# A gated pooling and forgetting-attention block: copies moved to ScalarE's queue, a store deferred, V's transposes in another bank, buffers shifted by 128 bytes, and another pacing

## The chip, the cores and the metric

The kernel runs on one core of one Trainium2 chip. The metric is device time in microseconds (us) of one execution. A core has five engines that run their own instruction streams in order: TensorE (PE, matmuls; its weight loads are listed apart as PEld), VectorE (DVE), ScalarE (ACT), GpSimd (POOL) and SyncE (SP, which here only issues DMA transfers). They meet through semaphores. The profile also gives the clock that was granted to TensorE, as a share of full speed.

## The reference

One hybrid decoder block on 1024 tokens of width 1024, with 16 learned meta tokens put ahead of them, all in float32:

```python
h = rmsnorm(concat(meta, x), norm_g)
u_pool, z_pool, q, k, v, z_attn, f_logit, g_pool, g_attn = split(h @ w_in)
y_pool = causal_multiscale_pool(u_pool, pool_w, pool_scale) * silu(z_pool)
log_f = log_sigmoid(f_logit + b_forget)
# 8 heads of 64; logit[t, s] = q_t.k_s / 8 + sum of log_f over s < j <= t, causal, softmax
y_attn = forgetting_attention(q, k, v, log_f) * silu(z_attn)
merged = sigmoid(g_pool) * (y_pool @ w_up_pool) + sigmoid(g_attn) * (y_attn @ w_up_attn)
out = rmsnorm(h_in + merged @ w_out, final_norm_g)[:, 16:]
```

## The kernel before

**Numbers.** Each operand of a large matmul is split into a rounded high part and the rest (hi and lo), and a product is three matmuls: hi by hi, hi by lo, lo by hi (`g_mm3`, L167). ACT makes the high parts (L158), POOL most low parts (L160).

**Stages.** First the normalised input is transposed into `hh` and `hl` (hi and lo) and the first pair of heads gets its q, k and v. Then comes attention, up to about 442 us of the profiled execution. After it come the gate products (L1034), the two up-projections (`up`, L1234) and the output product (`prod`, L1350). The gate products and the output product are a seven-product scheme on quarter matrices of 512 by 512, so that sums and differences of quarters are needed. These sums are made in DRAM during attention: a copy puts one quarter into a *sum buffer* (`GS`, `TD`, `HS`), and an adding transfer issued by POOL adds another (`add`, L609). `SUMS` (L639) lists by unit which copies (`put`, `put_g`, `put_h`, and `put_neg`, which first negates a block of the input) and additions are issued.

**Attention.** It is cut into 16 units: four pairs of heads, two heads each, two halves of 512 queries. A unit has 5 blocks of 128 keys (first half) or 9 (second half); blocks on the diagonal are narrower. For each block, `qk` (L689) makes the scores in a PSUM bank, which ACT and DVE move to the tile S with bias and mask, and DVE keeps a running maximum. `maxes` (L720) turns that into one maximum per query, with two 32-by-32 transposes on DVE and small copies on ACT. `soft` (L739) subtracts the maximum (DVE), takes the exponential (ACT), splits it into ph (ACT) and pl (DVE), and adds it into `acc` for the row sums (POOL). `av` (L762) multiplies ph and pl by V, two blocks later. The score blocks of unit i+1 are merged with the softmax blocks of unit i (`merged`, L782). At the end of a unit `finish` (L769) stores the output and `acc`.

**Filler.** PE's order is written out by the program. Between attention's blocks a filler (`Fill`, L370) hands PE projections: q, k, v of the next pair of heads, which must be done by a given unit, and others that are stored for later (u and gates, `f_u` L358 and `f_raw` L348; their results go through the two `st` buffers to DRAM). After each block, `merged` calls `F.pull(PACE * dve - pe)`: `dve` is the planner's estimate of the VectorE time of that block in ns, `pe` the TensorE time of the block, and the filler then issues matmuls of that nominal duration (`mm_ns`). Further pulls stand around the maxima (`LM1`, `LM2`) and ahead of a unit's last two `av` (`TAIL`). The order on the other engines is made by the scheduler of the framework from the program's order, its dependences and hand-written orders (`after`).

**Banks.** Of the eight PSUM banks, `pj` has two, `pk` one, `psT` two, `psS` two, `psO` one. During attention the projections alternate over the two of `pj` (`fill_bank`, L183, with `spare` false), and the scores over the two of `psS` and the one of `pk` (`third`, L177). V is projected transposed in three pieces of columns (`f_v`, L337), and blocks of it are turned by TensorE (`v_blocks`, L308) into a bank taken by `fill_bank`.

**Memory.** SBUF is given out in order: `cst`, `wp` (weight splits), `gp` (q, k and other large tiles), `stg` (the `st` buffers), `sm` (small), then `ap` (attention: S, V, acc, ph, pl) and later in its place `bp` (gate weights `gw`, za, zp and others). `hh` and `hl`, and later `hq` (operands of the later products), lie at the other end. `PADS` puts unused bytes into `cst` (`lead`) and `sm` (`rest`).

Of the kernel before, what the change touches and what calls it, by code (L numbers as in the profile page):

```python
# [22 lines left out]
KB = 128  # L23
# [4 lines left out]
COL_F, COL_GP, COL_GA = 3072, 3080, 4104  # L28
PIECES = ((0, 384), (384, 768), (768, 1040))
HROW = 1088  # L30
PADS = {"lead": 32, "rest": 0}
HALVES = ((0, 512), (512, 1024))
PJ, PT = 2, 2
PACE = 1.05
LATENCY = 1800.0
LAT2 = 1600.0
LM1, LM2 = 1400.0, 1800.0
TAIL = 900.0
FIRST = 2200.0
NPH = 3  # L40
LAG = 2
# [9 lines left out]
def mm_ns(n):  # L51
    return max(n * 0.4219, 107.0)
# [3 lines left out]
def tile_hybrid_block(ctx, tc, x, meta, norm_g, w_in, b_forget, pool_w, pool_scale,  # L56
                      w_up_pool, w_up_attn, w_out, final_g, out):
    nc = tc.nc
# [124 lines left out]
    def fill_bank():  # L183
        return third(pj, "pj") if spare[0] else pj.tile([128, 512], F32, name="pj")
# [121 lines left out]
            V[p, e] = ap_.tile([KB, NB, 2, 64], F32R, name="V", bufs=3)  # L306

    def v_blocks(p, *parts):  # L308
        pt = fill_bank().rearrange("p (n e d) -> p n e d", e=2, d=64)
        n = 0  # L310
        for b0, b1 in parts:
            for b in range(b0, b1):
                nc.tensor.transpose(pt[:, n], VT[p][:, KS[b]:KS[b] + KB], ident)
                n += 1
                yield 109.0
        for e in range(2):
            n = 0
            for b0, b1 in parts:
                pv = pt[:, n:n + b1 - b0]
                n += b1 - b0  # L320
                vh = V[p, e][:, b0:b1, e, :]
                nc.scalar.activation(vh, pv[:, :, e, :], AF.Copy)
                nc.vector.tensor_tensor(V[p, e][:, b0:b1, 1 - e, :], pv[:, :, e, :], r32(vh), op=ALU.subtract)
# [89 lines left out]
    F = Fill()  # L413
# [185 lines left out]
    def rows_of(t):  # L599
        return t.rearrange("(k p) c -> p k c", p=128)  # L600

    def put(dst, src):
        after(nc.sync.dma_start(dst, src), stores[-1])

    def put_g(dst, src):
# [13 lines left out]
    def put_neg(blk, k, *dsts):  # L619
        t = ap_.tile([128, 512], F32, name="neg", bufs=2)  # L620
        after(nc.scalar.activation(t, hblock(hh4, blk)[:, k], AF.Copy, scale=-1.0), exps[-1])
        for c in range(0, 512, 256):
            sub = nc.gpsimd.tensor_tensor(t[:, c:c + 256], t[:, c:c + 256], hblock(hl4, blk)[:, k, c:c + 256],
                                          op=ALU.subtract)
            after(sub, accs[-1])
        for d in dsts:
            put(HS[d][128 * k:128 * k + 128], t)

    def n21(k):
        put_neg("21", k, "X", "A")  # L630
# [38 lines left out]
    class Unit:  # L669
# [9 lines left out]
        def a_steps(self):  # L679
            for b in range(self.nb):  # L680
                w = 512 - self.c0[b]
                yield w, 0.8 * w + 110 + 250 * (b * KB + KB > self.t0), 2 * mm_ns(w), (lambda b=b: self.qk(b))

        def c_steps(self):
            for b in range(self.nb):
                w = 512 - self.c0[b]
                yield w, 2.8 * w + 390, 2 * mm_ns(w), (lambda b=b: self.soft(b))

        def qk(self, b):  # L689
            p, e, q0, t0, kb, c0 = self.p, self.e, self.q0, self.t0, self.kb[b], self.c0[b]  # L690
# [48 lines left out]
        def soft(self, b):  # L739
            kb, c0 = self.kb[b], self.c0[b]  # L740
            s = self.S[b]
            if b == 0:
                self.po = psO.tile([128, 512], F32, name="po")
                self.acc = ap_.tile([KB, 512], F32, name="acc", bufs=2)
            nc.vector.tensor_tensor(s[:kb, c0:], s[:kb, c0:], self.pm[:kb, c0:], op=ALU.subtract)  # L745
            exps.append(nc.scalar.activation(s[:kb, c0:], s[:kb, c0:], AF.Exp))  # L746
            ph = ap_.tile([128, 512], F32R, name="ph", bufs=NPH)
            pl = ap_.tile([128, 512], F32R, name="pl", bufs=NPH)
            nc.scalar.activation(ph[:kb, c0:], s[:kb, c0:], AF.Copy)  # L749
            dves.append(nc.vector.tensor_tensor(pl[:kb, c0:], s[:kb, c0:], r32(ph[:kb, c0:]), op=ALU.subtract))  # L750
            self.P[b] = (ph, pl)
            acc, S0 = self.acc, self.S[0]
            if b == 1:
                if c0:
                    nc.gpsimd.tensor_copy(acc[:, :c0], S0[:, :c0])
                accs.append(nc.gpsimd.tensor_tensor(acc[:, c0:], S0[:, c0:], s[:, c0:], op=ALU.add))  # L756
            elif b > 1:
                accs.append(nc.gpsimd.tensor_tensor(acc[:kb, c0:], acc[:kb, c0:], s[:kb, c0:], op=ALU.add))  # L758
            if b >= LAG:
                self.av(b - LAG)  # L760
# [8 lines left out]
        def finish(self):  # L769
            hr, lr = rows(self.e)  # L770
            po, acc = self.po, self.acc
            t = ap_.tile([128, 512], F32, name="t")
            if self.p == 3:
                nc.scalar.activation(t[hr], po[lr], AF.Copy)
                nc.vector.tensor_tensor(t[hr], po[hr], t[hr], op=ALU.add)
            else:
                nc.scalar.activation(t, po, AF.Copy)
            for n, part in (("y", hr), ("y2", lr))[:1 if self.p == 3 else 2]:
                nc.sync.dma_start(spill[n, self.p][hr, self.q0:self.q0 + 512], t[part])
            nc.sync.dma_start(accd[:, 4 * self.p + 2 * self.e + self.half], acc)  # L780

    def merged(a, c):  # L782
        out_ = []
# [37 lines left out]
    for i, u in enumerate(units):  # L821
        nxt = units[i + 1] if i + 1 < 16 else None
        F.now = i
        if nxt is not None and nxt.p != u.p:
            F.until(f"q{nxt.p}", f"k{nxt.p}")
        merged(list(nxt.a_steps()) if nxt else [], list(u.c_steps()))
        for b in range(u.nb - LAG, u.nb):
            F.pull(TAIL)
            u.av(b)
        if i == 1:  # L830
            after(nc.scalar.activation(pwh, pw, AF.Copy), exps[-1])
            nc.gpsimd.tensor_tensor(pwl, pw, r32(pwh), op=ALU.subtract)
        if nxt is not None:
            nxt.maxes(hook=lambda tr: sums_at(i, tr))
        u.finish()
        if i == 12:
            g_raw0 = [gp.tile([128, 2, 512], F32, name="graw", tag="g") for _ in range(2)]
            for k in range(2):
                put(g_raw0[k], rows_of(GSRC[0][0])[:, 2 * k:2 * k + 2])
        if i == 14:  # L840
            g_w0 = [[gp.tile([128, 2, 512], F32R, name="gw0", tag="g") for _ in range(2)] for _ in range(2)]
            for k in range(2):
                after(nc.scalar.activation(g_w0[0][k], g_raw0[k], AF.Copy), exps[-1])
                for c in range(0, 2):
                    for h0 in (0, 256):
                        after(nc.gpsimd.tensor_tensor(g_w0[1][k][:, c, h0:h0 + 256], g_raw0[k][:, c, h0:h0 + 256],
                                                      r32(g_w0[0][k][:, c, h0:h0 + 256]), op=ALU.subtract), accs[-1])
        if nxt is not None and nxt.p != u.p:
            F.until(f"v{nxt.p}")
            pair_fill(nxt.p + 1)  # L850
    F.drain()
    last_dve = dves[-1]
    A.close()
# [620 lines left out]
```

## Time and profile before

| what | value |
|---|---|
| time, median of 3 runs | 741.27 us (741.16 to 744.6) |
| time of the profiled execution | 742.0 us |
| its span, first to last instruction | 740.3 us |
| mean granted TensorE clock | 0.993 |
| PE busy | 714.7 us (97%) |
| PEld busy | 612.2 us (83%) |
| DVE busy | 521.7 us (70%) |
| ACT busy | 426.3 us (58%) |
| POOL busy | 336.2 us (45%) |
| DMA | 134.08 MB, mean 181 GB/s |

Busy time of PE includes the overlap of matmuls that follow each other in the pipeline, so a matmul's listed mean (some 390 ns at 512 columns) is longer than the distance to the next one. A window row gives the stretch, then for each engine its busy us and instructions (x), then the granted clock, the share of the DMA engines and GB/s. A group row gives line, engine, operation, output and inputs, shape, count, then busy us and mean ns of one, then the engine's idle time before it and what ended it. A timeline row gives start, duration and instruction, with the idle time before it in brackets. A chain row gives start, duration and group.

### The profile page before, as it was taken

How to read it: one execution, taken by the hardware profiler on the slowest of the kernel's cores; microseconds unless marked ns; L12 is line 12 of the kernel's file. 1: busy time of each engine (PE TensorE's matmuls, PEld its weight loads, DVE VectorE, ACT ScalarE, POOL GpSimd, SP SyncE). 2: the span in 40 equal slices, each digit the busy share in tenths (PEclk: the TensorE clock that was granted, in tenths of full speed). 3: DMA queues.
4: the chain of work that ended last, by engine and by line, in shares of the span. 5: the costliest groups of instructions: out<-in, count | busy, mean ns of one | idle time of the engine just before them, and what ended most of it. 6: DMA issues, size and time to landing. Idle time of an engine off the chain costs nothing.

```text
span 740.3 us, 10889 instructions
## 1 busy us (share of the span) xinstructions
PE 714.7 (97%) x3613; PEld 612.2 (83%) x3613; DVE 521.7 (70%) x917; ACT 426.3 (58%) x944; POOL 336.2 (45%) x417
## 2 busy tenths in 40 slices
PE   8999999698999899998999999999999999999996
PEld 6997999597779888897788887888888888888885
DVE  5743479376777867888686894889756654887775
ACT  7653477465796766776666733436544522626445
POOL 5412337446465764657356763355953011006243
PEclk9999999899999999999999999999999999999998
DMA  9211252854989759494888879889605557672006
GB/s 303 60 29 30 73 167 89 247 141 140 300 227 244 197 143 248 128 283 124 234 219 215 224 182 349 298 220 328 182 28 178 177 185 268 218 270 69 0 1 227
DMA packets 97226, 134.08 MB, mean 181 GB/s; under 512 B 11569, under 2 KB 62769, under 8 KB 94914
## 3 DMA queue, kind: packets, MB, share of 16 engines
q1 hardware_dynamic: 93360, 112.42, 47.5%
q0 software_dynamic: 2512, 18.35, 12.9%
q10 hardware_dynamic: 1298, 2.63, 0.9%
q8 instruction: 28, 0.46, 0.2%
q14 instruction: 28, 0.23, 0.1%
HBM read 103.29 MB, written 62.59 MB: 224 GB/s over the span
## 4 chain that ended last, share of the span: by engine, by line
PE 72%; ACT 9%; DVE 7%; DMA 2%; issue 2%; POOL 1%; POOLq 0%; SPq 0%; ACTq 0%; DVEq 0%
PE pj L172 38%; PE pj L1034 12%; PE pj L1354 8%; PE pt L1034 4%; PE po L766 4%; PE pt L1354 2%; ACT S L746 2%; DMA sp_u<-st 2%; ACT ph L749 1%; PE ps L705 1%; PE ps L704 1%; ACT S L709 1%; PE pj L529 1%; DVE pl L750 1%; DVE S L745 1%
## 5 line engine op out<-in xcount | busy, mean ns | idle before, releaser
L172 PE MATMUL pj<-hh,whi 128*128 128x512 f32 (+3 forms) x576 | 130.5, 354 | 7.9 <-ACT vt L302 5.1
L172 PE MATMUL pj<-hh,wlo 128*128 128x512 f32 (+3 forms) x576 | 129.1, 348 | 0.3 <-POOL wlo L447 0.3
L172 PE MATMUL pj<-hl,whi 128*128 128x512 f32 (+3 forms) x576 | 128.0, 346 | 0.0
L172 PEld LDWEIGHTS pj<-hh,whi 128*128 128x128 f32 x576 | 96.8, 191 | 20.7 <-ACT vt L302 6.3
L160 POOL TENSOR_TENSOR wlo<-raw,whi 128x256 fp32r<-128x256 f32 x100 | 75.9, 798 | 68.1 <-ACT whi L158 33.4
L172 PEld LDWEIGHTS pj<-hh,wlo 128*128 128x128 f32 x576 | 97.1, 190 | 9.5 <-POOL wlo L447 0.5
L172 PEld LDWEIGHTS pj<-hl,whi 128*128 128x128 f32 x576 | 96.5, 188 | 9.2
L750 DVE TENSOR_TENSOR pl<-S,ph 128x512 fp32r<-128x512 f32 (+4 forms) x112 | 88.1, 797 | 22.6 <-ACT ph L749 21.9
L758 POOL TENSOR_TENSOR acc<-acc,S 128x272 f32<-128x272 f32 (+4 forms) x80 | 77.3, 967 | 16.9 <-ACT S L746 11.8
L996 POOL TENSOR_TENSOR gw<-graw,gw 128x256 fp32r<-128x256 f32 x52 | 50.0, 984 | 47.6 <-ACT gw L991 45.2
L1034 PE MATMUL pj<-gh,gw 128*128 128x512 f32 x276 | 65.8, 395 | 0.0
L1034 PEld LDWEIGHTS pj<-gh,gw 128*128 128x128 f32 x276 | 52.0, 188 | 12.2
L749 ACT ACTIVATE ph<-S 128x512 fp32r<-128x512 f32 (+4 forms) x112 | 52.8, 480 | 10.3 <-PE po L766 8.2
L746 ACT ACTIVATE S<-S 128x512 f32<-128x512 f32 (+4 forms) x112 | 49.8, 478 | 13.2 <-DVE S L745 13.2
L718 DVE TENSOR_TENSOR pt<-pt,S 128x400 f32<-128x400 f32 (+2 forms) x96 | 46.6, 486 | 8.8 <-ACT S L709 5.5
L745 DVE TENSOR_TENSOR S<-S,pt 128x512 f32<-128x512 f32 (+4 forms) x112 | 50.3, 497 | 0.5
L1247 DVE TENSOR_TENSOR rl<-pj,rl 128x512 f32<-128x512 f32 x32 | 22.0, 689 | 28.7 <-PE pj L172 28.1
L991 ACT ACTIVATE gw<-graw 128x512 fp32r<-128x512 f32 x38 | 23.6, 626 | 31.1 <-DMA graw<-gs 9.2
L709 ACT ACTIVATE S<-ps,negc 128x512 f32<-128x512 f32 (+4 forms) x63 | 31.8, 517 | 13.1 <-PE ps L705 12.6
L766 PE MATMUL po<-pl,V 128*128 128x512 f32 (+4 forms) x112 | 37.6, 335 | 1.0 <-DVE pl L750 1.0
L756 POOL TENSOR_TENSOR acc<-S 128x400 f32<-128x400 f32 (+1 forms) x16 | 20.9, 1306 | 37.9 <-ACT S L746 33.1
L1354 PE MATMUL pj<-opw 128*128 128x512 f32 (+1 forms) x168 | 36.2, 374 | 0.0
(246 smaller groups left out, 1411.7 us busy)
## 6 DMA issues: line engine op xcount, KB each, us to landing
raw<-in_w_in_dram SPq DMA_DIRECT2D x27, 512.0 KB, 7.2
gs<-gs POOLq DMA_DIRECT2D x4, 1536.0 KB, 13.5
graw<-gs SPq DMA_DIRECT2D x12, 512.0 KB, 6.7
gs<-in_w_in_dram SPq DMA_DIRECT2D x5, 1024.0 KB, 11.9
td<-in_w_out_dram SPq DMA_DIRECT2D x5, 1024.0 KB, 12.7
graw<-in_w_in_dram SPq DMA_DIRECT2D x9, 512.0 KB, 5.4
xt<-in_x_dram SPq DMA_DIRECT2D x8, 512.0 KB, 7.5
accd<-acc SPq DMA_DIRECT2D x16, 256.0 KB, 3.2
```

The lines of the kernel that those rows point to most:

```text
L160: ins = nc.gpsimd.tensor_tensor(lo[:, k:k + 2], raw[:, k:k + 2], r32(hi[:, k:k + 2]), op=ALU.subtract)
L172: nc.tensor.matmul(ps, a, b, start=(i == 0), stop=(i == len(seq) - 1))
L718: nc.vector.tensor_tensor(m[:kb, c0:], m[:kb, c0:], s[:kb, c0:], op=ALU.max)
L745: nc.vector.tensor_tensor(s[:kb, c0:], s[:kb, c0:], self.pm[:kb, c0:], op=ALU.subtract)
L746: exps.append(nc.scalar.activation(s[:kb, c0:], s[:kb, c0:], AF.Exp))
L749: nc.scalar.activation(ph[:kb, c0:], s[:kb, c0:], AF.Copy)
L750: dves.append(nc.vector.tensor_tensor(pl[:kb, c0:], s[:kb, c0:], r32(ph[:kb, c0:]), op=ALU.subtract))
L758: accs.append(nc.gpsimd.tensor_tensor(acc[:kb, c0:], acc[:kb, c0:], s[:kb, c0:], op=ALU.add))
L766: nc.tensor.matmul(self.po[:, c0:], v, r[:kb, c0:], start=(b == 0 and i == 0), stop=(b == self.nb - 1 and i == 1))
L996: nc.gpsimd.tensor_tensor(op[:, 1, k:k + 2], raw[:, k:k + 2], r32(op[:, 0, k:k + 2]), op=ALU.subtract)
L1034: nc.tensor.matmul(ps, stat(n, i, p, k), op_h[n][q][k // 2][:, k % 2], start=fresh and m == 0, stop=m == 11, skip_group_check=True)
L1354: nc.tensor.matmul(ps, pick(A_, k, p)[:, i * 128:(i + 1) * 128], pick(B_, k, q)[:, c0:c1], start=start and n == 0, stop=n == 11, skip_grou ...
```

## The change

Six edits. (1) `put` no longer issues a copy on SP but keeps it in a list; the copies of the list are issued on ACT's queue when `soft` has issued the exponential of block 1 of the next unit, in order behind it. `put_now` is the old `put`; the negated blocks and two loads of raw gate weights still use it. (2) The store of `acc` is kept back and issued by SP at block 2 of the next unit's softmax (the last one after the loop). (3) `v_blocks` takes a score bank once attention has begun. (4) `PADS["rest"]` is 128 bytes in place of 0. (5) The planner's estimates of a block's time, `PACE`, `LM2` and the pull ahead of the last two `av` are other numbers. (6) `TAIL` goes, as `LATENCY` stands in its place.

```diff
-PADS = {"lead": 32, "rest": 0}
+PADS = {"lead": 32, "rest": 128}
-PACE = 1.05
+PACE = 1.32
 LATENCY = 1800.0
-LM1, LM2 = 1400.0, 1800.0
-TAIL = 900.0
+LM1, LM2 = 1400.0, 3200.0
...
     def v_blocks(p, *parts):
-        pt = fill_bank().rearrange("p (n e d) -> p n e d", e=2, d=64)
+        pt = (fill_bank() if spare[0] else third(psS, "ps")).rearrange("p (n e d) -> p n e d", e=2, d=64)
...
+    puts, held = [], []
+
     def put(dst, src):
+        puts.append((dst, src))
+
+    def put_now(dst, src):
         after(nc.sync.dma_start(dst, src), stores[-1])
...
         for d in dsts:
-            put(HS[d][128 * k:128 * k + 128], t)
+            put_now(HS[d][128 * k:128 * k + 128], t)
...
-                yield w, 0.8 * w + 110 + 250 * (b * KB + KB > self.t0), 2 * mm_ns(w), (lambda b=b: self.qk(b))
+                yield w, 1.04 * w + 70, 2 * mm_ns(w), (lambda b=b: self.qk(b))
...
-                yield w, 2.8 * w + 390, 2 * mm_ns(w), (lambda b=b: self.soft(b))
+                yield w, 1.75 * w + 130, 2 * mm_ns(w), (lambda b=b: self.soft(b))
...
             exps.append(nc.scalar.activation(s[:kb, c0:], s[:kb, c0:], AF.Exp))
+            while b == 1 and puts:
+                after(nc.scalar.dma_start(*puts.pop(0)), exps[-1])
+            while b == 2 and held:
+                nc.sync.dma_start(*held.pop(0))
...
-            nc.sync.dma_start(accd[:, 4 * self.p + 2 * self.e + self.half], acc)
+            held.append((accd[:, 4 * self.p + 2 * self.e + self.half], acc))
...
-            F.pull(TAIL)
+            F.pull(LATENCY)
...
-                put(g_raw0[k], rows_of(GSRC[0][0])[:, 2 * k:2 * k + 2])
+                put_now(g_raw0[k], rows_of(GSRC[0][0])[:, 2 * k:2 * k + 2])
...
+    nc.sync.dma_start(*held.pop(0))
     F.drain()
```

## The prediction

> **What bounds the kernel now.** I read the page's busy table and slices first, then the windows, then PE's waits and SP's queue in the attention stage.
>
> ```profile
> PE 714.7 (97%) x3613; PEld 612.2 (83%) x3613; DVE 521.7 (70%) x917; ACT 426.3 (58%) x944; POOL 336.2 (45%) x417
> PEclk9999999899999999999999999999999999999998
> 137.85:145.00 7.15, 0.39 (x2) 0.00 (x0) 1.29 (x2) 2.71 (x7) 1.22 (x2) 0.82 1.03 321
> 145.00:149.20 4.20, 4.20 (x12) 4.00 (x13) 2.89 (x5) 4.20 (x10) 2.98 (x5) 0.50 0.75 240
> 450.00:553.00 103.00, 102.94 (x443) 83.49 (x444) 80.24 (x80) 51.66 (x81) 59.84 (x62) 1.00 0.75 230
> 570.00:657.00 87.00, 87.00 (x385) 72.03 (x385) 55.95 (x82) 36.71 (x50) 5.78 (x8) 1.00 0.66 225
> ```
>
> PE sets the time. From the gate products on (450 us) it never stops, so there the change can only alter how long one matmul takes. Before that, in the sixteen units of attention, PE loses time in places: once (first window row) for 7.15 − 0.39 = 6.8 us, after which the clock is 0.50 for 4.2 us, another 2.1 us. That one event costs **8.9 us**. Most other losses stand behind V's transposes.
>
> **V's transposes (L309).** Projections and V's blocks share the two banks of `pj`. A V chunk runs piece 0 in bank A, piece 1 in B, transposes in A, so piece 2 needs B, which has only just been filled:
>
> ```profile
> 168.37 0.38 PE L313 MATMUL pj<-ident,vt 128*128 128x128 f32 x2
> 170.33 0.47 ACT L302 ACTIVATE vt<-pj 128x384 f32<-128x384 f32 x1
> 170.85 1.02 PE L172 MATMUL pj<-hh,whi 128*128 128x272 f32 x6 [2.10 <-ACT vt L302]
> 171.82 0.28 ACT L322 ACTIVATE V<-pj 128x128 fp32r<-128x128 f32 x1 [0.86 <-DVE V L323]
> ...
>   PE pj L172: 5.1, 4
> ...
> 363.34 0.98 PE L172 MATMUL pj<-hh,whi 128*128 128x512 f32 x3 [0.78 <-ACT st L355]
> ```
>
> The row with 5.1, 4 (who waited for `vt`) sums four such waits; the last row is a fifth of 0.78, also behind transposes. With the transposes in a score bank the projections alternate A, B, A and each eviction has a whole piece of cover (24 matmuls of 227 ns, the figure below, are 5.4 us, three quarters of that at 384 columns). Removed: 5.1 + 0.8 = 5.9 us. Added: a score bank held from 168.37 to about 172.1, some 3.7 us. Three banks rotate over the scores, so only the third score tile behind it can wait. A five-block unit merges nine score tiles into its softmax of 12.9 us (401.20 to 414.10, below), shorter with less filler: three in some 3 to 4 us. So up to 1 us, at about three places: 0 to 3 us. I take 0.5, near the lower end, since most V blocks lie in nine-block units, with five score tiles over 18 us. Term: **−5.4** (bounds −5.9 and −2.9).
>
> **Buffers 128 bytes higher.** The memory map of the program puts `wp` and `hq` at 224 bytes past a multiple of 256, and `ap` and `bp` (V, ph, pl, gw) at 96; `rest` lies below `ap` and `bp` and moves them to 224 as well.
>
> ```profile
> L1034 PE MATMUL pj<-gh,gw 128*128 128x512 f32 x276 | 65.8, 395 | 0.0
> L1354 PE MATMUL pj<-opw 128*128 128x512 f32 x142 | 32.8, 389 | 0.0
> L172 PE MATMUL pj<-yh,whu 128*128 128x512 f32 x64 | 17.1, 389 | 0.0
> L172 PE MATMUL pj<-plh,pwh 128*128 128x512 f32 x8 | 3.1, 393 | 0.0
> L766 PE MATMUL po<-ph,V 128*128 128x512 f32 x48 | 19.0, 395 | 0.0
> ...
> 458.68 8.36 PE pj L1034 x36
> 668.13 8.16 PE pj L1354 x36
> ```
>
> Same shape, same clock: where weights and moving operand both start at 224 (L1354, L172 with yh) the mean is 389 ns, and 36 matmuls take 8.16 us, 226.7 ns each. Where one of them starts elsewhere (gw and V at 96, plh at 32 or 160) it is 393 to 395, and 36 take 8.36 us, 232.2 each. The gate product has 504 matmuls, of which 456 read gw from `bp`: 456 × 5.5 = 2.5 us. P·V has 2 × 112 (the row shows 48 full ones of one half), many narrower: at most 224 × 5.5 = 1.2; I take 0.8. Term: **−3.3** (bounds −3.7, and 0 if the address is not the cause).
>
> The Trainium skill, SBUF — State Buffer, "Who interferes with whom", says that PE waits for no other engine at SBUF, and its page has no price for where an operand starts. By it this term is 0 and the sum 4.9 us down rather than 8.2. No row here shows another cause for the 5.5 ns, so I keep the rows.
>
> **Copies on ScalarE's queue, acc stored later.** What is late at 131 to 145 us:
>
> ```profile
> SPq L780 <- POOL acc L758: 89.6, 12, 14.2
> ...
> 124.83 0.32 SPq L780 DMA_DIRECT2D accd<-acc  x1
> 126.09 4.82 SPq L153 DMA_DIRECT2D raw<-in_w_in_dram  x2
> 131.00 1.02 SPq L367 DMA_DIRECT2D sp_u<-st  x2
> 132.07 0.59 SPq L603 DMA_DIRECT2D hsX<-neg  x1
> 132.71 0.70 SPq L603 DMA_DIRECT2D hsA<-neg  x1
> 133.46 1.25 SPq L603 DMA_DIRECT2D gs<-in_w_in_dram  x2
> 134.82 5.58 SPq L779 DMA_DIRECT2D sp_y<-t  x1
> ...
> 130.44 1.07 POOL L611 DMA_DIRECT2D hs<-hsl  x1
> 142.29 0.40 ACT L365 ACTIVATE st<-pj 128x272 f32<-128x272 f32 x1 [8.00 <-DMA sp_u<-st]
> ```
>
> SP waits for acc, then for the weight buffers, and the two spills of u leave together only at 131.00, beside the adding transfer that POOL issues at 130.44. ACT stands 8.00 us, to 142.29, for the staging buffer that the first of them frees, and everything behind it. The change takes two things out of that queue: the acc store, issued by SP a unit later when acc is long complete (12 waits, 89.6 us; behind it stood weight loads, spills and `sp_y`), and the copies. The weight loads, which stand ahead of the spills and wait for POOL, and the adding transfer stay. So the event may vanish (−8.9) or stay (0); with two of three reasons for lateness gone I take half, **−4.5**.
>
> What it adds: ACT now issues 20 copies (4 of hh and hl, 10 of weights to gs, 5 to td, 1 from A to B), each after the second exponential of a unit. Behind each stand ph, the next exponentials and the evictions that free banks for PE.
>
> ```profile
> 186.22 0.48 SPq L603 DMA_DIRECT2D hs<-hh  x1
> 186.80 0.55 SPq L603 DMA_DIRECT2D hsl<-hl  x1
> 187.44 5.98 SPq L779 DMA_DIRECT2D sp_y<-t  x2
> 196.18 3.13 SPq L603 DMA_DIRECT2D gs<-in_w_in_dram  x2
> ...
> gs<-in_w_in_dram SPq DMA_DIRECT2D x5, 1024.0 KB, 11.9
> ```
>
> On SP one costs 0.48 to 0.65 us, so 20 × 0.56 = 11.2 us of ACT, about 1.2 us in a unit with two. ACT has room (17.64 of 22.60 us and 13.41 of 18.00, below), and PE has filler queued. Bounds 0 and 11.2; I take **+2**. The copies go out some 4 us later in a unit and land 11.9 us after that; the earliest adding transfer that reads one comes a unit later (18.00 us, below, or more), so POOL waits little or not. Moved acc stores cost nothing: acc has two buffers and the third user is a unit further on.
>
> **Older pacing.** Filler asked per full softmax block: before 1.05 × (2.8 × 512 + 390) − 432 = 1483 ns, after 1.32 × (1.75 × 512 + 130) − 432 = 922; per score block 114 (376 on the diagonal) becomes 363. Summed over a nine-block unit with the five score blocks merged into it: 12.1 us becomes 7.2; a five-block unit 6.6 becomes 5.0. The two pulls at a unit's end grow from 2 × 0.9 to 2 × 1.8, the pulls about the maxima from 1.4 + 1.8 to 1.4 + 3.2. Nine-block unit: 17.1 to 15.4; five-block: 11.6 to 13.2. A pair keeps 28.7, so the stage's matmuls are the same and filler is not used up early: only its place moves, from the softmax loop to the maxima and the end.
>
> ```profile
> 288.00:310.60 22.60, 22.60 (x106) 18.81 (x105) 19.25 (x36) 17.64 (x41) 14.27 (x16) 1.00 0.60 164
> 291.80:310.10 18.30, 18.30 (x86) 15.16 (x85) 16.36 (x29) 15.98 (x34) 12.03 (x12) 1.00 0.50 116
> 374.80:397.40 22.60, 22.60 (x107) 18.88 (x106) 16.94 (x34) 15.58 (x37) 16.49 (x17) 1.00 0.90 237
> 397.40:415.40 18.00, 18.00 (x87) 15.14 (x87) 13.48 (x29) 13.41 (x32) 12.72 (x19) 1.00 0.89 226
> 401.20:414.10 12.90, 12.90 (x62) 10.88 (x61) 9.79 (x20) 11.44 (x25) 9.79 (x15) 1.00 0.98 257
> ```
>
> Rows one and three are nine-block units from one maxima transpose to the next, row two the softmax part of the first, rows four and five a five-block unit and its softmax part. A nine-block unit takes PE 22.6 us and would take 22.6 − 1.7 × 1.05 = 20.8 (a full matmul counts 216 ns to the planner and takes 227). DVE is busy 19.25 and 16.94 of it and idles 1.4 in the maxima chain ((22.60 − 18.30) − (19.25 − 16.36)) and 1.9 in softmax (18.30 − 16.36), which I count as latency that stays: 22.5 and 20.2. So some of these eight units become DVE's: 1.7 us for one like the first, 0 for one like the second. Five-block units get longer on PE and lend nothing back. Upper bound 8 × 1.7 = 13.6. Lower bound: a gain of 2 where ACT's splits behind the maxima now get more cover. I take 0.4 a unit, **+3**, nearer the low end, since PE reaches softmax some 3 us later (0.9 + 0.9 + 1.4) and starts with that lead.
>
> **Sum.** −5.4 − 3.3 − 4.5 + 2 + 3 = −8.2. The profiled execution has 742.0 us (span 740.3 and 1.7 around it), 0.7 above the median 741.27. So 733.8 on that scale, **733** beside the median. Differences under 0.5% (3.7 us) count as no change.
>
> **Rivals.**
> *ACT's queue held (slower).* A transfer that cannot be issued holds its queue: 5.98 us for two `sp_y` behind 1 MB copies, 5.58 for another, and two gs copies took 3.13 where a pair took 1.25. SP can afford it; ACT can't. If a copy stands 6 us on ACT early in softmax, PE's lead of some 3 us (pacing, above) covers half and 3 us are lost. Above 4 of the 13 units with copies (4 × 3 = 12) the gain of 8.2 and the 3.7 of the margin are gone. With five: 733 + 15 = 748. For: ACT's copies now leave as the adding transfers start, and those slowed SP's queue to 5.58 for one issue. Against: ACT's ring holds nothing but these. Chance 0.20.
>
> *No change.* The event stays because the loads stand ahead of the spills as before, and DVE takes 6 us rather than 3: 733 + 4.5 + 3 = 740.5. Here the change doesn't do what it says: the freed SP queue moves nothing. Chance 0.20. The Trainium skill, DMA: Bandwidth & Descriptors, "Issuing engines are not separate DMA queues", speaks for it: transfers from all queues share the same 16 engines, and a second issuer saves only issue time. By it the −4.5 is 0 and the time 737.5, with pacing as I have it. The trace agrees so far: the spills crawled beside a transfer of another queue.
>
> *All of it.* The event goes (−4.4 more), pacing and issue cost nothing (−5): 723.6. Chance 0.17.
>
> The forecast's own case, 729 to 737, has 0.43. Chances: faster 0.43 + 0.17 = 0.60, same 0.20, slower 0.20. The range reaches from the whole gain, 723, to five held units, 748.
>
> **What would show it.** V: no wait of PE's L172 for `vt`; if score matmuls (L704) wait for V instead, that step is wrong. Address: L1034 and L766 at 389 ns, 36 gate matmuls in 8.16 us; at 395 it was not the address. Event: no stretch with a clock of 0.50 in attention, and no wait of `st` for `sp_u`. Issue: ACT's copies at 0.5 us each; several over 2 us mean the first rival. Pacing: nine-block units near 21 us with waits of P·V (L766) for `pl`. A time above 745 would make the prediction wrong in its direction.

## The result, and the profile after

The changed kernel takes **725.29 us** (median of 4 runs, 724.43 to 725.45) against 741.36 us before: a ratio of 0.9771, 95% interval 0.9743 to 0.9799. That is 16 us faster. The forecast was 733, faster by 8: the direction was right, and the gain is twice the one forecast. The nearest of the cases was the rival "all of it" (723.6).

The profiled execution after took 725.36 us (span 723.7, clock 0.997). Line numbers have moved by up to 9: L172 is now L171, L704 and L705 are L708 and L709, L766 is L774, L1034 is L1043, L1354 is L1363. First the page, then five windows (columns as before), then PE's waits in attention (60 to 442 us; total us, times, longest us), then the chain that ended last.

```profile
PE 709.6 (98%) x3613; PEld 610.1 (84%) x3613; DVE 515.9 (71%) x917; ACT 425.4 (59%) x944; POOL 333.1 (46%) x417
PEclk9999999999999999999999999999999999999998
L1043 PE MATMUL pj<-gh,gw 128*128 128x512 f32 x276 | 64.2, 389 | 0.0
```

```profile
128.00:150.00 22.00, 21.74 (x138) 20.96 (x137) 13.80 (x30) 12.74 (x35) 12.06 (x18) 1.00 0.93 260
272.60:295.70 23.10, 22.21 (x103) 18.37 (x102) 19.13 (x38) 17.86 (x41) 15.72 (x17) 1.00 0.56 160
358.80:379.50 20.70, 20.70 (x99) 17.33 (x98) 17.52 (x34) 14.97 (x36) 13.38 (x13) 1.00 0.94 259
379.50:399.10 19.60, 19.60 (x94) 16.35 (x93) 13.61 (x30) 14.00 (x33) 16.06 (x23) 1.00 0.83 225
433.00:536.00 103.00, 103.00 (x455) 85.07 (x454) 79.39 (x79) 52.49 (x81) 59.09 (x60) 1.00 0.74 225
```

```profile
PE pj L708 <- DVE V L322: 1.5, 1, 1.5
PE ps L708 <- DVE S L717: 1.3, 2, 1.0
PE po L774 <- DVE pl L758: 1.0, 2, 0.7
PE ps L708 <- ACT S L713: 0.4, 1, 0.4
```

```profile
477.20 8.16 PE pj L1043 x36
...
640.62 8.16 PE pj L1363 x36
```

What the reader is to see: the dip in the clock row is gone, and in 128 to 150 us, where PE once stood for 6.8 us, it is busy for 21.74 of 22.00 at full clock. No wait for `vt` is left. In the gate products 103 us now hold 455 matmuls where they held 443, and 36 of them take 8.16 us, as in the output product. The nine-block units (second and third window) take 23.1 and 20.7 us, the five-block one 19.6. PE's waits in attention add up to 4.6 us; two of them, 0.2 us each, are not shown.

ACT's copies are issued as follows; the stall of 8 us for the staging buffer has become two smaller ones that PE doesn't feel:

```profile
131.94 1.03 POOL L615 DMA_DIRECT2D hs<-hsl  x1
...
133.22 0.60 ACTq L752 DMA_DIRECT2D gs<-in_w_in_dram  x1
133.95 0.81 ACTq L752 DMA_DIRECT2D gs<-in_w_in_dram  x1
143.31 0.49 ACT L364 ACTIVATE st<-pj 128x384 f32<-128x384 f32 x1 [2.61 <-DMA sp_u<-st]
149.21 0.49 ACT L364 ACTIVATE st<-pj 128x384 f32<-128x384 f32 x1 [3.71 <-DMA sp_u<-st]
```

### The profile page after: what moved, and what is told of

The parts are those of the page before. It is cut to its first block, busy times and chain, and to the rows that moved or that the text cites. A ratio compares the mean times of both kernels' runs of the same rounds, so it can differ in the third digit from the quotient of the medians.

```text
span 723.7 us, 10860 instructions
## 1 busy us (share of the span) xinstructions
PE 709.6 (98%) x3613; PEld 610.1 (84%) x3613; DVE 515.9 (71%) x917; ACT 425.4 (59%) x944; POOL 333.1 (46%) x417
## 3 DMA queue, kind: packets, MB, share of 16 engines
q0 software_dynamic: 2512, 18.35, 13.7%
## 4 chain that ended last, share of the span: by engine, by line
PE 85%; DVE 4%; ACT 4%; issue 1%; ACTq 0%; POOLq 0%; POOL 0%; DVEq 0%
PE pj L171 48%; PE pj L1043 12%; PE pj L1363 8%; PE po L774 4%; PE pt L1043 4%; PE pt L1363 2%; PE ps L709 2%; PE ps L708 2%; PE pj L528 1%; DVE pl L758 1%; PE pj L709 1%; PE pj L708 1%; DVE ql L273 1%; ACT qa L269 1%; ACT ph L757 1%
## 5 line engine op out<-in xcount | busy, mean ns | idle before, releaser
L171 PE MATMUL pj<-hh,whi 128*128 128x512 f32 (+3 forms) x576 | 128.0, 349 | 0.3 <-DVE ka L296 0.2
L171 PE MATMUL pj<-hh,wlo 128*128 128x512 f32 (+3 forms) x576 | 127.1, 346 | 0.2 <-POOL wlo L446 0.2
L171 PE MATMUL pj<-hl,whi 128*128 128x512 f32 (+3 forms) x576 | 127.3, 346 | 0.0
L159 POOL TENSOR_TENSOR wlo<-raw,whi 128x256 fp32r<-128x256 f32 x100 | 73.8, 767 | 80.5 <-ACT whi L157 34.0
L171 PEld LDWEIGHTS pj<-hh,whi 128*128 128x128 f32 x576 | 97.5, 190 | 11.0 <-PE pj L171 0.5
L171 PEld LDWEIGHTS pj<-hh,wlo 128*128 128x128 f32 x576 | 96.6, 188 | 10.3 <-POOL wlo L446 0.5
L171 PEld LDWEIGHTS pj<-hl,whi 128*128 128x128 f32 x576 | 96.7, 189 | 9.6
L758 DVE TENSOR_TENSOR pl<-S,ph 128x512 fp32r<-128x512 f32 (+4 forms) x112 | 84.4, 764 | 20.3 <-ACT ph L757 19.5
L766 POOL TENSOR_TENSOR acc<-acc,S 128x272 f32<-128x272 f32 (+4 forms) x80 | 76.2, 953 | 28.3 <-ACT S L750 23.1
L1043 PE MATMUL pj<-gh,gw 128*128 128x512 f32 x276 | 64.2, 389 | 0.0
L1043 PEld LDWEIGHTS pj<-gh,gw 128*128 128x128 f32 x276 | 51.8, 188 | 10.8
L774 PE MATMUL po<-pl,V 128*128 128x512 f32 (+4 forms) x112 | 38.1, 340 | 1.3 <-DVE pl L758 1.0
L713 ACT ACTIVATE S<-ps,negc 128x16 f32<-128x16 f32 (+4 forms) x65 | 33.0, 514 | 8.4 <-PE ps L709 7.5
L774 PE MATMUL po<-ph,V 128*128 128x512 f32 (+4 forms) x112 | 36.5, 326 | 0.2 <-ACT ph L757 0.2
L1363 PE MATMUL pj<-opw 128*128 128x512 f32 (+1 forms) x168 | 36.2, 374 | 0.0
```

Source lines behind the costliest of these rows:

```text
L159: ins = nc.gpsimd.tensor_tensor(lo[:, k:k + 2], raw[:, k:k + 2], r32(hi[:, k:k + 2]), op=ALU.subtract)
L171: nc.tensor.matmul(ps, a, b, start=(i == 0), stop=(i == len(seq) - 1))
L774: nc.tensor.matmul(self.po[:, c0:], v, r[:kb, c0:], start=(b == 0 and i == 0), stop=(b == self.nb - 1 and i == 1))
L1043: nc.tensor.matmul(ps, stat(n, i, p, k), op_h[n][q][k // 2][:, k % 2], start=fresh and m == 0, stop=m == 11, skip_group_check=True)
L1363: nc.tensor.matmul(ps, pick(A_, k, p)[:, i * 128:(i + 1) * 128], pick(B_, k, q)[:, c0:c1], start=start and n == 0, stop=n == 11, skip_grou ...
```

## The experiments

The theory after the result: each part acts by its own cause, the parts add up, and the stall at 131 to 145 us vanished because the copies and the acc store left SP's queue. The rivals: another part removed the stall; or pacing and issue, forecast at +5 together, had the other sign.

### One part at a time, on the kernel before

**Address alone.**

```diff
-PADS = {"lead": 32, "rest": 0}
+PADS = {"lead": 32, "rest": 128}
```

> The kernel before with the 128 unused bytes alone. Theory 1 (where an operand starts sets the rate of a matmul): gate products L1034 go from a mean of 395 ns to 389, 36 of them from 8.36 us to 8.16; the time falls by 2.5 (gate products) to 3.7 us, to 738. Rival (the rate has another cause, such as the stage's order or the traffic): 395 ns stay and the time stays at 741.

Measured: 738.14 us against 740.89, ratio 0.9957 (0.9942 to 0.9972): **−2.8**. The group of the gate products:

```profile
L1034 PE MATMUL pj<-gh,gw 128*128 128x512 f32 x276 | 64.2, 389 | 0.0
L766 PE MATMUL po<-ph,V 128*128 128x512 f32 x48 | 18.9, 394 | 0.0
```

In the gate products the 5.5 ns follow the address and nothing else in the change. P·V (second row, 395 before) hardly moves, although V, `ph` and `pl` were shifted by the same 128 bytes.

**The score bank for V's transposes alone.**

```diff
-        pt = fill_bank().rearrange("p (n e d) -> p n e d", e=2, d=64)
+        pt = (fill_bank() if spare[0] else third(psS, "ps")).rearrange("p (n e d) -> p n e d", e=2, d=64)
```

> The kernel before with V's transposes in a score bank alone. Theory 1: PE's waits for vt in L172 (5.1 us) go, at most 0.5 us of new waits of the score matmuls come, and the time falls by some 5 us to 736; the stall of 8.9 us at 131 to 145 us stays. Rival (score tiles wait for the bank): waits of 2 to 3 us at the score matmuls, time 738 to 739. Rival 2 (the stall at 131 us hangs on any shift in time): the clock of 0.50 is gone and the time is 727.

Measured: **727.18 us**, ratio 0.9808 (0.9792 to 0.9824), 13.7 us less. One line of code makes most of the gain, and rival 2 of this run is the one that held: the stall is gone, with SP's queue as it was. The stretch of the stall, PE's longest wait, and the issues of the two transfers:

```profile
131.00:149.20 18.20, 18.20 (x116) 17.66 (x116) 12.77 (x28) 12.82 (x35) 7.51 (x11) 1.00 1.01 307
```

```profile
PE pj L704 <- DVE V L323: 2.5, 2, 2.3
```

```profile
129.71 1.08 POOL L611 DMA_DIRECT2D hs<-hsl  x1 [0.48 <-DVE mt L723]
129.72 1.01 SPq L367 DMA_DIRECT2D sp_u<-st  x2
```

Before, the adding transfer was issued at 130.44 and the two spills (the stores of u from the `st` buffers to DRAM, `sp_u`) 0.56 us after it; here both go out together. The spills' time from issue to landing (last column, the median in us) between 126 and 146 us, first before, then here:

```profile
sp_u<-st SPq DMA_DIRECT2D x2, 192.0 KB, 11.0
```

```profile
sp_u<-st SPq DMA_DIRECT2D x3, 192.0 KB, 4.8
```

So the stall seemed to hang on half a microsecond between two queues, which a change anywhere ahead of it can shift.

**Copies on ACT's queue and acc stores later, alone.**

```diff
     def put(dst, src):
+        puts.append((dst, src))
...
+            while b == 1 and puts:
+                after(nc.scalar.dma_start(*puts.pop(0)), exps[-1])
+            while b == 2 and held:
+                nc.sync.dma_start(*held.pop(0))
```

> The kernel before with the 20 copies on ScalarE's queue and the acc stores a unit later, and nothing else. Theory 1 (SP's full queue made the spills late): no stretch at a clock of 0.50 in attention, ACT's wait of 8 us for the staging buffer goes, time 732 to 733 (8.9 us less, at most 2 back for the issues on ACT). Rival (pacing or the bank removed that stall): the stall stays and the time is 741 to 743.

Measured: 740.79, ratio 0.9995 (0.9984 to 1.0006): nothing. ACT's wait of 8.00 us for `st` is gone, yet PE stands again: it goes on at 147.26, where it was 145.00 before. ACT's timeline, then PE's:

```profile
138.92 0.59 ACTq L755 DMA_DIRECT2D gs<-in_w_in_dram  x1
...
145.03 0.50 ACTq L755 DMA_DIRECT2D gs<-in_w_in_dram  x1
145.58 0.60 ACT L723 ACTIVATE pt<-S 128x512 f32<-128x512 f32 x1 [5.27 <-DMA sp_u<-st]
```

```profile
147.26 0.80 PE L711 MATMUL pj<-qa,ka 128*128 128x512 f32 x1 [4.59 <-ACT S L716]
```

The last ACT row reads as if `pt` waited for a spill of u, which it doesn't touch. What waited is the instruction ahead of it, the second copy, issued at 145.03. In the program every transfer counts up one of eight semaphores in turn, for SP and ACT together, and waits until the transfer that used it before has landed; the one ahead of this copy on its semaphore is a spill of u. The trace bears this out: the copy and the spill that SP issued at 133.50 name the same semaphore, and that spill landed at 145.01, just before the copy went out. So ACT stood some 5 us for a transfer of SP's queue that was itself held by the adding transfer. This is the prediction's first rival, at one place.

**Older pacing alone.** (`PACE`, `LM2`, the estimates of a block, and 1800 in place of 900 in the last pull.)

```diff
-PACE = 1.05
+PACE = 1.32
-LM1, LM2 = 1400.0, 1800.0
+LM1, LM2 = 1400.0, 3200.0
-TAIL = 900.0
+TAIL = 1800.0
-                yield w, 0.8 * w + 110 + 250 * (b * KB + KB > self.t0), 2 * mm_ns(w), (lambda b=b: self.qk(b))
+                yield w, 1.04 * w + 70, 2 * mm_ns(w), (lambda b=b: self.qk(b))
-                yield w, 2.8 * w + 390, 2 * mm_ns(w), (lambda b=b: self.soft(b))
+                yield w, 1.75 * w + 130, 2 * mm_ns(w), (lambda b=b: self.soft(b))
```

> The kernel before with the older pacing alone (estimates of a block's time, PACE, LM2, TAIL at 1800). Theory 1 (pacing costs nothing and removes nothing): 741, within 2 us; the 8.9 us stall stays. The prediction's step: 3 us slower, 744, with nine-block units bound by DVE. Rival (pacing removed the stall, because the u projections fall at another time against the adding transfers): 732, no clock of 0.50 in attention.

Measured: 740.92, ratio 0.9991 (0.9967 to 1.0016), single runs 734.28 to 743.89. No change, but not for the reason expected: the stall at 131 us is gone, and another stands 100 us later. ACT, then PE:

```profile
245.67 0.60 ACT L777 ACTIVATE t<-po 128x512 f32<-128x512 f32 x1 [10.55 <-DMA sp_y<-t]
```

```profile
248.39 1.95 PE L172 MATMUL pj<-hh,whi 128*128 128x272 f32 x7 [10.54 <-ACT vt L302]
```

What ACT waits for is the store of an output (`sp_y`). SP began to issue it at 217.03 and got it out some 18 us later, beside an adding transfer that POOL had issued at 215.66 (`gs<-gs`, 18.6 us to landing); then the next one ran beside it (`hsX<-hs`, issued at 233.30, 10.8 us to landing). Which of the two held it is not shown; with all adding transfers left out (below) this stall is gone too. A zero was the sum of a gain and a loss. One of the ten runs took 734.28 us at a granted clock of 0.996, the others 737 us or more at 0.992 or less: it may be a run without the stall; the trace is of one with it. The four parts alone give −2.8, −13.7, 0 and 0, and all of them −16: they add up only by accident, as the next runs show.

### The changed kernel less one part, and two parts together

**V's transposes back in a projection bank.** (The `v_blocks` line as before.)

> The changed kernel with V's transposes back in a projection bank; address, queue and pacing as changed. Theory A (the bank is worth only its own waits for vt, some 5 us; the 9 us stall goes or stays by a matter of about 1 us between the spill of u and the adding transfer): two outcomes, 731 without such a stall anywhere, or 739 to 740 with one, at 131 to 145 us or elsewhere in attention, and in either some 5 us of waits for vt. Theory B (the bank itself removes the stall): the stall is back and the time is 738 to 740, with ACT held 5 us or more at a buffer that a transfer frees.

Measured: 729.95 us, ratio 0.9846 (0.9825 to 0.9867), with no stall of this kind. PE waits as before:

```profile
PE pj L172 <- ACT vt L302: 5.6, 4, 2.5
```

The bank itself is worth 729.95 − 725.29 = **4.7 us** here, theory A's first outcome (731). It isn't needed to remove the stall at 131 to 145 us.

**Copies and acc stores back on SP.** (Part 3 undone.)

> The changed kernel with copies and acc stores on SP's queue as before. If the queue part costs nothing and brings nothing: 725, within 1 us of the changed kernel. If the 20 issues on ACT cost what the prediction took: 723. If SP's shorter queue is what keeps the stall away in the changed kernel: 733, with a stretch at a low clock in attention.

Measured: 732.66, ratio 0.9871 (0.9830 to 0.9913), single runs from 727.82 to 734.71. By its time this is the third outcome, but the stall at 131 to 145 us stays away, with SP's queue as it was; what has come back is the one of the older pacing, where PE waits for ACT, which waits for `sp_y`:

```profile
246.27 0.90 PE L313 MATMUL ps<-ident,vt 128*128 128x128 f32 x3 [6.63 <-ACT vt L302]
```

**The pacing of before.** (Part 5 undone.)

> The changed kernel with the pacing of before. If pacing costs nothing: 725, within 1 us. If it costs the 3 us of the prediction: 722. If it gives what the others don't (fewer waits of P.V): 727 or more.

Measured: 727.03, ratio 0.9805 (0.9779 to 0.9830). Taken alone this says that the older pacing brings 1.7 us. The trace says otherwise: ACT's second copy waits for a spill again (5.17 us, PE 4.49 us, at 143 us), as in the run with the queue part alone.

**Address and bank alone, on the kernel before.** (The first two diffs above.)

> The kernel before with the 128 bytes and the score bank for V's transposes, and nothing else. If these two are the whole gain and add up: 727.2 - 2.8 = 724.4, as fast as the changed kernel or 1 us faster. If the queue part or pacing is needed beside them: 726 or more.

Measured: **724.14 us**, ratio 0.9765 (0.9745 to 0.9786). Two of the parts give the whole gain; with the queue part and pacing it is 1.2 us slower, which these intervals don't separate from nothing.

### What makes the stall

**Without one adding transfer, then without all of them.** In `SUMS`:

```diff
-        4: [(add, HS["22"], HS["l22"]), (n21, 3), (put_g, GS[3], GB["22"])],
+        4: [(n21, 3), (put_g, GS[3], GB["22"])],
```

> The kernel before without one adding transfer: HS[22] += HS[l22] of unit 4 (issued at 130.44 us) isn't done, so that quarter lacks its low part. Theory A (the spills of u are held by the packets of that transfer, and ACT with them): no wait of 8 us for the staging buffer, no low clock at 141 to 149 us, and the time is 732 (8.9 us less), unless the next adding transfer makes such a stall. Theory B (SP's late issue of the spills makes the stall): the stall and 741 stay.

Measured: 741.76, ratio 1.0010 (0.9996 to 1.0023). The stall stayed, but the trace shows why that decides nothing: POOL still issues `hs<-hsl` (at 129.61). The transfer at that place is that of unit 1, not of unit 4; the run had taken out the wrong one.

```diff
     def add(dst, src):
...
-        behind(nc.gpsimd.dma_start(d, r, accum_op=ALU.add, max_dma_last_dim=8192), trs[-1])
```

> The kernel before without all of the sixteen adding transfers into the sum buffers (the quarter sums lack their second terms; the copies stay). Theory A: no stall of this kind can occur anywhere, 732 or a little less, and this is the kernel before without its stall. Theory B: 741.

Measured: **733.63 us**, ratio 0.9902 (0.9887 to 0.9916); there are fourteen such transfers, not sixteen. The stall is gone and nothing replaces it. The 7.7 us are the stall and whatever else these fourteen transfers cost. Who used the DMA engines in the kernel before, from 134 to 139 us and from 140 to 145 us (packets, MB, share of 16 engines; q0 is POOL's queue, q1 is SP's):

```profile
q0 software_dynamic: 109, 0.89, 93.2%
q1 hardware_dynamic: 142, 0.18, 11.4%
```

```profile
q1 hardware_dynamic: 1097, 1.88, 103.2%
q0 software_dynamic: 2, 0.01, 0.8%
```

While the adding transfer runs, in packets of 8 KB, SP's queue moves a tenth of what it moves right after (0.18 MB against 1.88). By number of packets the two queues are not far apart (109 against 142); a packet of the adding transfer is some six times as large (8 KB against 1.3 KB). Spills that haven't left by then land when it does, at 142.0 us. The Trainium skill, DMA: Bandwidth & Descriptors, "Issuing engines are not separate DMA queues", says that transfers of all engines run on the same 16 DMA engines and interleave; the trace agrees on the first, and shows the interleaving as very uneven.

**The right transfer, a unit later.** Nothing is left out.

```diff
-        1: [(add, HS["11"], HS["l11"]), (n21, 0), (put_g, GS[1], GB["11"])],
-        2: [(n21, 1), (put_g, GS[5], GB["12"])],
+        1: [(n21, 0), (put_g, GS[1], GB["11"])],
+        2: [(add, HS["11"], HS["l11"]), (n21, 1), (put_g, GS[5], GB["12"])],
```

> The kernel before with the adding transfer that goes out at 130.44 us (by its place in the trace it is HS[11] += HS[l11] of unit 1) issued a unit later; all else and the output are as before. Theory A (the stall at 131 to 145 us is made by this one transfer's packets getting ahead of the two spills of u): the stall there goes, and the time is 733, as without all adding transfers, unless the later transfer meets other spills. Theory B (any order of SP's queue makes it): 741, the stall stays at 131 to 145 us.

Measured: **734.81 us**, ratio 0.9897 (0.9861 to 0.9934). SP's queue and its order are as before, its spills go out at 130.24, POOL's transfer at 148.99, and the stall is gone:

```profile
148.99 1.08 POOL L611 DMA_DIRECT2D hs<-hsl  x1 [4.23 <-PE po L766]
```

That is 7.0 us less than before, so this one transfer beside the spills made the stall.

How the score bank removes it is argued from the traces, not shown by a run that moves the two issues and nothing else. In all nine kernels that have SP's queue as before and this transfer in its place, the spills go out behind it at one of two distances. Five have them 0.56 to 0.58 us behind, and PE stands 5.7 to 6.8 us (before, address alone, the run above that left out the wrong transfer, and the two on addresses below). Four have them 0.01 to 0.21 us behind, and there is no stall at this place (bank alone, address and bank, older pacing alone, the changed kernel without its queue part). In these four POOL first waits 0.29 to 0.48 us for the maxima's transpose on DVE (`mt`, as in the row with [0.48 <-DVE mt L723]); in the five it does not. So by these traces it is decided by whether POOL's issue is held back at that point, and bank and older pacing each happen to hold it.

### Queue and pacing, apart from the stall

With the adding transfers left out no stall of that kind can hide a part's own worth.

> Copies on ScalarE's queue and acc stores later, again without the adding transfers. Against the kernel before without them it shows what this part costs or brings apart from the stall: +2 by the prediction's term, 0 if the issues are hidden under PE's work.

Measured: 734.11 us (733.87 to 735.10) against 733.63 (733.47 to 735.32): the queue part costs **+0.5**, not to be told from 0. One event beside the part itself is in it: the trace with the queue part has 3.5 us at a clock of 0.51 (242.0 to 245.5 us) behind a wait of 2.12 us for `vt`, some 1.7 us of lost time, while the one without it has a wait as long (2.11 us) and no such stretch. By this estimate the part would gain about 1 us without it.

> The older pacing, again without the adding transfers. Against the kernel before without them it shows what pacing costs apart from the stall: +3 by the prediction's term, 0 if DVE doesn't bind the nine-block units, below 0 if the fuller cover behind the maxima pays.

Measured: 730.23 (730.07 to 731.04) against 733.63: older pacing **gains 3.4** on the kernel before. PE's waits, first with the pacing of before, then with the older:

```profile
PE pj L172 <- ACT vt L302: 5.1, 4, 2.1
PE pj L172 <- ACT st L355: 1.8, 3, 0.8
PE po L765 <- DVE pl L749: 1.0, 1, 1.0
```

```profile
PE pj L172 <- ACT vt L302: 4.7, 4, 1.7
PE po L765 <- DVE pl L749: 1.9, 4, 0.6
...
PE pj L172 <- ACT st L355: 0.2, 1, 0.2
```

It takes away waits of the projections for evictions (5.1 + 1.8 becomes 4.7 + 0.2) and adds waits of P·V for `pl` (1.0 becomes 1.9). The first are the waits that the score bank removes too. Hence the next pair, the changed kernel and the changed kernel with the pacing of before, both without the adding transfers:

> The changed kernel without the fourteen adding transfers into the sum buffers (the quarter sums lack their second terms). It has no such stall to lose, so 724 to 725; below 722 would mean that these transfers cost the changed kernel time in another way.

> The changed kernel with the pacing of before, again without the adding transfers. If pacing is worth 3.4 us whatever the bank (as it was without the bank): 728. If pacing and the bank remove the same waits: 724 to 725, no difference from the changed kernel without these transfers. If pacing costs the 3 us of the prediction once the bank is there: 721 to 722.

Measured: 725.38 (723.92 to 725.54) and **721.21** (720.97 to 722.25). Once the bank is there, the older pacing **costs 4.2 us**: its gain has nothing left to take away. In the lists of PE's waits (first with the older pacing) one sees part of it:

```profile
PE pj L707 <- DVE V L322: 1.5, 1, 1.5
PE po L773 <- DVE pl L757: 1.0, 2, 0.6
PE ps L707 <- DVE S L716: 1.0, 1, 1.0
PE ps L707 <- ACT S L712: 0.4, 1, 0.4
```

```profile
PE po L776 <- DVE pl L760: 1.1, 3, 0.6
PE ps L710 <- DVE S L719: 1.0, 1, 1.0
PE pj L710 <- DVE V L323: 0.4, 1, 0.4
```

The waits for V's eviction on DVE and for ACT's scores are longer, 1.5 us together. The profiled spans differ by 722.2 − 719.3 = 2.9 (the profiled run with the older pacing was the fastest of its four); the lists don't hold the rest. Waits for `pl` are alike, so the step "DVE bounds the nine-block units" isn't shown by them.

### What of an address counts

```diff
-PADS = {"lead": 32, "rest": 0}
+PADS = {"lead": 32, "rest": 160}
```

> The kernel before with 160 unused bytes in place of 0, so that gw, V, ph and pl start at a multiple of 256 bytes, not at 224 past one like the other operand. If it matters that both operands start at the same place modulo 256: L1034 at 395 ns as before. If any start but 96 will do: 389 ns.

```diff
-PADS = {"lead": 32, "rest": 0}
+PADS = {"lead": 160, "rest": 128}
...
+    low = ctx.enter_context(tc.tile_pool(name="low", bufs=1, side="right"))
+    low.tile([128, 32], F32, name="low", bufs=1)
     hp = HX.enter_context(tc.tile_pool(name="hp", bufs=1, side="right"))
```

> The kernel before with unused bytes placed so that weights, hidden operands and the gate weights all start 96 bytes past a multiple of 256 (128 bytes more below the weights, 128 bytes at the other end, 128 in rest). If equal starts of both operands modulo 256 are what counts: L1034 at 389 ns, L1354 at 389 too, time about 738. If the place 224 itself counts: L1034 at 395 ns or more and L1354 up to 395, time 741 to 750.

Measured: with gw at 0 and the other operand at 224, then with both at 96 (the places are those of the program's memory map; the runs show what the moves do):

```profile
L1034 PE MATMUL pj<-gh,gw 128*128 128x512 f32 x276 | 66.0, 395 | 0.0
...
457.39 8.40 PE pj L1034 x36
```

```profile
L1036 PE MATMUL pj<-gh,gw 128*128 128x512 f32 x276 | 64.2, 389 | 0.0
L1356 PE MATMUL pj<-opw 128*128 128x512 f32 x144 | 33.3, 389 | 0.0
```

One run each, 741.18 and 738.38 us. A round address doesn't help and 224 is nothing special: it is the **common start** of weights and moving operand, here modulo 256; no run tells 256 from another step. For P·V no run shows it.

### A version that beats both

The changed kernel with the pacing of before (4.2 us), and, against the stall that then comes back, the first adding transfer a unit later (the diff above).

> The changed kernel with the pacing of before and the first adding transfer (HS[11] += HS[l11]) issued a unit later; complete, with the reference's output. If pacing costs 4 us once the score bank is there and the one stall that then comes back (141 us, 5 us of ACT) is made by that adding transfer: 721 to 722, some 4 us below the changed kernel. If the transfer meets other spills a unit later: 725 to 727, no gain.

Measured: **721.42 us** (721.08 to 722.24), ratio to before 0.9728 (0.9708 to 0.9748), 3.9 us below the changed kernel and 5.6 below the same without the moved transfer (727.03). Nothing is left out of the computation. POOL issues the moved transfer at 148.34, and ACT waits nowhere in attention for a spill of u.

## Why the prediction was right or wrong

By its own terms, in us, with the sum against 741.3:

| term | forecast | measured | from |
|---|---|---|---|
| V in a score bank | −5.4 | −6.7 (pacing of before; against a kernel without the adding transfers), −4.7 (older pacing) | 733.63 − 2.75 − 724.14; 729.95 − 725.29 |
| buffers 128 bytes higher | −3.3 | −2.8 | 738.14 against 740.89 |
| the stall at 131 to 145 us | −4.5 | −7.7 (all adding transfers left out), −7.0 (one of them moved) | 733.63 against 741.36; 734.81 against 741.81 |
| issue on ACT and older pacing | +2 and +3 | +1.2 together | 725.29 − 724.14 |
| sum | −8.2 | −16.0 | |

The measured sum takes the parts in one order, with the first figure of each row; in another order the terms differ, as the second figures show. Of the 7.8 us that the forecast lacks, 3.2 lie in the stall, 3.8 in issue and pacing and 1.3 in the bank; the address takes 0.5 back.

**V's transposes: right in sign and mechanism.** The waits for `vt` went, and all 1.8 us of those for `st` with them, of which the prediction had counted 0.8. With the older pacing the size is within the bounds (−5.9 and −2.9), with the pacing of before beyond them. Score matmuls do wait for V's eviction, which the prediction named as a sign that this step is wrong: 1.5 us in the changed kernel and 2.5 with the bank alone, against 0.5 taken and 3 as the bound. They are fewer than the waits that went, so the step holds. PE's lists hold only part of the gain: their waits fall by 3.8 us, from 10.0 (before, without the adding transfers) to 6.2 (address and bank).

**Address: right for the gate products**, row by row (389 ns, 8.16 us), and they carry it. The 0.8 us given to P·V is not to be seen, and its sign, L766 at 389 ns, did not come (394). The Trainium skill's page SBUF — State Buffer, "Who interferes with whom", by which the term would be 0, calls PE's reads of the moving operand and of the weights independent; the 5.5 ns that hang on where these two start differ from that, and the measurement decides.

**The stall: the failed step.** "With two of three reasons for lateness gone I take half", −4.5, where 7.0 to 7.7 us went. The two reasons that the change takes away weren't the cause. With copies and acc stores off SP's queue the time stays (740.79), and PE stands at nearly the same place; moving one adding transfer removes the stall (734.81), with SP's queue untouched. The prediction had that transfer in its rows, at 130.44 beside spills at 131.00, counted it among what stays, and didn't ask how close the race was. By the traces of the nine kernels it was a matter of about half a microsecond, which the bank and the older pacing, two parts that the prediction had not connected with it, each win. That it went was luck by the prediction's own reasoning. A value of half was a mean of two outcomes, neither of which was half.

**Issue on ACT: mis-sized, with its rival seen.** The 20 issues took 0.37 to 1.13 us each in the changed kernel, about as forecast, but they cost PE little or nothing (+0.5 rather than +2, and a gain beside the bank, below). The first rival, ACT held some 6 us by a copy that can't be issued, did occur, at one place (5.27 and 5.17 us), in the two kernels that had the queue part with the pacing of before and every adding transfer in its place; in the changed kernel the two copies at that place went out at 133.22 and 133.95, on semaphores whose earlier transfers had landed. The order of the program gave them these and not the one of the late spill: luck again, as nothing in the change sees to it. "ACT's ring holds nothing but these", said against it, was wrong: its transfers share eight semaphores with SP's.

**Older pacing: right only in company.** The +3 is 4.2 with the score bank, and −3.4 without. The prediction worked out each part against the trace of before and added them; the pacing's gain and the bank's removed the same waits. That it costs through DVE isn't shown, and the prediction's bound didn't show it either: 19.25 + 1.4 + 1.9 = 22.5 us adds to DVE's work all the time that DVE idled in the same unit, which gives the unit's own length (22.6) back, whatever bounds it. Its sign, nine-block units near 21 us with waits of P·V for `pl`, came by half: they take 23.1 and 20.7 us, and these waits are 1.0 us as before. Nor is it shown why the queue part, worth nothing alone, goes with a gain of 2.7 to 2.9 us beside the bank: 721.21 without the adding transfers and 721.42 with them against 724.14 for address and bank alone. A wait of the scores for V's eviction that is shorter (0.4 us against the 2.5 of the bank alone, rows above) would make up most of it; why it is shorter stays open.

**The direction came and the number did not.** The rival "all of it" joined "the event goes" to "pacing and issue cost nothing", and had 0.17. Its two halves were priced as if the first hung on SP's queue alone.

## What to carry to other kernels

A stall that hangs on which of two transfers goes first is won or lost whole, by any shift ahead of it: cost it as all or nothing, look for the next place where it can reappear, and remove it by moving the transfer itself. Test parts apart with that stall switched off, or a gain and a loss will look like zero, as they did for pacing (−3.4, +4.2, 0). Where a row says that an instruction waited for a transfer that it doesn't touch, look at the DMA issue ahead of it on its queue.

## What the runs showed that was not expected

- An adding transfer issued by POOL took 93% of the DMA engines' time in 8 KB packets from 134 to 139 us and left SP's queue a tenth of what it moved from 140 to 145, so that spills of 192 KB landed 11.0 us after their issue, against 4.8.
- A copy on ACT can be held by a transfer of SP: 5.2 us, through a semaphore that both use in turn.
- Matmuls of 512 columns stood 226.7 ns apart when weights and moving operand started at the same place modulo 256 (224 and 224, 96 and 96), and 232.2 (224 with 96) or 233.3 ns (224 with 0) where they didn't.
- A wait of PE of 2.1 to 2.3 us was followed by some 3.4 us at a clock of 0.50 in three traces (2.27 us with the bank alone, 2.10 with the moved transfer, 2.12 with the queue part without adding transfers) and by full clock in three others (2.10 before, 2.11 without adding transfers, 2.23 with address and bank). By this estimate equal waits cost 0 or some 1.7 us more, so single differences of that size need more than one run.
